# Gate products of a recurrent branch: full-array products with zero blocks, and pairs of 64-row products

## The chip, the cores and the metric

The kernel runs on one core of a Trainium2 chip. The metric is the device time of one execution in microseconds (us). The engines are named as in the profile: PE multiplies matrices, PEld is its weight load, DVE works on vectors, ACT evaluates functions and copies, POOL does small things, SP issues most transfers.

## The reference, cut to what matters

The program is one step of a two-layer backbone on 128 context tokens and 256 latent tokens (384 columns in all). Each layer has a pooling branch, an attention branch and a recurrent branch, then a feed-forward part. The change touches the two gates of the recurrent branch:

```python
xb = xf.reshape(b, l, LRU_BLOCKS, LRU_BLK)          # 8 blocks of 64 channels
rg = sigmoid(einsum('blnc,encd->eblnd', xb, wa) + ba)   # e: forward, backward
ig = sigmoid(einsum('blnc,encd->eblnd', xb, wx) + bx)
log_a = LRU_C * rg * log_sigmoid(lam)
a = exp(log_a)
inp = sqrt(-expm1(2 * log_a)) * ig * xf
hf, hb = linear_scan(a[0], inp[0]), linear_scan(a[1], inp[1], reverse)
```

Each gate is a product of a block of 64 channels with a 64 x 64 matrix. Everything is float32.

## The kernel before

Features lie on the 128 rows, tokens on the columns. A product in float32 precision is made of three products of rounded halves, `mm3` (L339): high weights by high data (L341), low weights by high data (L342), high weights by low data (L343). The weights come in chunks of 8 or 4 matrices of 128 x 128, in the order of `chunk_order` (L52). Each chunk is loaded to `raw` (L291), rounded to `whi` by ACT (L304) and its remainder is written to `wlo` by DVE (L313). Six buffers of each kind let this run ahead of the products.

Every engine works through its own instructions in the order in which the program was traced; `job` (L407) interleaves them by hand: the products of a chunk, then one stage of each evacuation that is still under way (`tick`), one step of the side work (`side_step`), then the first stage of its own evacuation, then some modulation steps on DVE (`after`, L261). PSUM has eight banks, taken in turn.

In each layer the first branch group (b = 0, the pooling branch) carries the recurrent gates. `lru_gates` (L603) is called for channel chunk c = 0, 1, 2 ahead of d = 2, 4, 6, and for c = 3 behind d = 7. Each chunk has 128 channels, so two blocks of 64. Before, the two 64 x 64 matrices of a gate stand on the diagonal of a 128 x 128 matrix whose other two quarters are zero. For each direction `e` there are two such matrices, so 2 x 3 products of 386 columns into two banks, `pa` and `px`. ACT takes both with a Tanh (L615 `th`, L616 `ti`), then computes `t2` (L619) and an Exp (L620); DVE has three operations (L622 to L624) in the next stage, ACT one more (L626) in the one after.

Behind the call for c = 3 the evacuations are flushed. Then the side work begins: `branch_lru_scan` starts with eight square roots on ACT (L634), then DVE multiplies (L648), scans (L655) and sums (L661, L662); `branch_attn` has, pair of heads by pair, transposes of v (L764), scores (L701: products of 64 rows, two heads side by side in two banks), a softmax on DVE and ACT (L714 to L736), transposes of its result (L743), copies out (ACT L749, DVE L752) and the products with v (L778, L783). The main stream of that time is the q, k and v products, whose banks ACT empties (L857).

Of the kernel before, what the change touches and what calls it, by code (L numbers as in the profile page):

```python
# [45 lines left out]
# products that warm the tensor engine up, around the first modulation vectors  # L46
WN = (8, 1, 1)
# modulation steps for each group of products, by part of the layer
# [3 lines left out]
def chunk_order():  # L52
    o = []
    for l in range(L):
        ms = [0, 1, 2, 3, 16, 17, 18, 19, 20, 21, 22, 23]
        if l == 0:
            ms = [m for m in ms if m not in FIRST0]
        o += [("in", l, m, 8) for m in ms]
        o += [("pw", l, 0, 4)]
        for b in (0, 2, 1):  # L60
            o += [("in", l, 24 + b * 8, 8)]
            for d in range(8):
                if b == 0 and d in (2, 6):
                    o += [("lru", l, d // 4, 8)]
                if d < 7:
                    o += [("in", l, 25 + b * 8 + d, 8)]
                o += [("br", l, b * 8 + d, 4)]
            if b == 0:
                for p in range(4):
                    o += [("in", l, 4 + p, 8), ("in", l, 8 + p, 8), ("in", l, 12 + p, 8)]  # L70
        o += [("wo", l, d, 8) for d in range(8)]
        for i in range(KF):
            o += [("fi", l, 2 * i, 8), ("fi", l, 2 * i + 1, 8)]
        for d in range(8):
            o += [("fo", l, 3 * d, 8), ("fo", l, 3 * d + 1, 8), ("fo", l, 3 * d + 2, 6)]
    return o
# [13 lines left out]
def emit(ctx, tc, A, outs):  # L90
# [33 lines left out]
    # silu(c), features on partitions, as the stationary side of small products  # L124
# [13 lines left out]
    # sel[p, s] = 1 where p = s modulo 32  # L138
# [3 lines left out]
    # 2h / count at the clipped ends of the pooling windows  # L142
    edge = cp.tile([128, 4, 2, 8], F32, name="edge")

    # additive mask of key columns, last column first
    cmask = cp.tile([128, 64], F32, name="cmask")

    def build_consts():
        ti = small("ti")
        G.iota(ti, pattern=[[1, 8]], base=0, channel_multiplier=0, allow_small_or_imprecise_dtypes=True)  # L150
        for g in range(4):
            h = float(1 << g)
            V.tensor_scalar(edge[:, g, 0], ti, h, None, op0=OP.add)
            V.tensor_scalar(edge[:, g, 1], ti, -1.0, 2 * h - 1, op0=OP.mult, op1=OP.add)
            yield
        V.tensor_scalar(edge[:, :, 1], edge[:, :, 1], 1.0, None, op0=OP.max)
        yield
        V.reciprocal(edge, edge)
        yield
        for g in range(4):  # L160
            V.tensor_scalar(edge[:, g], edge[:, g], 2.0 * (1 << g), None, op0=OP.mult)
            yield
        G.memset(cmask, 0.0)
        for rr in range(2):
            v = cmask[rr * 64:(rr + 1) * 64]
            # query column p, key column c = 63 - i: c >= min(p - 8, 48) and c < max(p - 8, 0) + 16
            G.affine_select(v[:, 16:64], v[:, 16:64], pattern=[[-1, 48]], base=55,
                            channel_multiplier=-1, compare_op=OP.is_ge, fill=NEG)
            G.affine_select(v[:, 0:48], v[:, 0:48], pattern=[[1, 48]], base=-56,
                            channel_multiplier=1, compare_op=OP.is_ge, fill=NEG)  # L170

    # derived per-channel parameters, both layers at once
# [3 lines left out]
    def build_dpar():  # L176
# [5 lines left out]
        # -log_sigmoid(lam) = max(-lam, 0) + log1p(z), z = exp(-|lam|)  # L182
# [13 lines left out]
        # log1p(z) = 2 atanh(z / (2 + z)), s <= 1/3  # L196
# [28 lines left out]
    def load_crow():  # L225
        # silu(c) * 2, broadcast over partitions
        Q.dma_start(out=crow, in_=A["crow"].unsqueeze(0).to_broadcast([128, 2, D]))
# [102 lines left out]
    def w_ahead(done, full=False):  # L330
        """traced before the products with the last `done` chunks, which still hold their tiles"""
        n = ws["use"] + NH - done
        w_lo(min(ws["cv"], n))
        w_hi(n)
        if full or done > 2:
            w_lo(n if full or done > 3 else n - 1)
        w_dma(min(n + NR, ws["lo"] + NR))
# [7 lines left out]
    def split_from(src, n=NT, scale=1.0, name="s"):  # L345
        """float32 data in SBUF or PSUM (times scale) -> two float32r tiles"""
        hi, lo = heap(name + "h", F32R), heap(name + "l", F32R)
        S.activation(hi[:, :n], src, AF.Copy, scale=scale)
        if isinstance(scale, float) and scale == 1.0:
            V.tensor_tensor(lo[:, :n], src, hi[:, :n].bitcast(F32), op=OP.subtract)  # L350
        else:
            V.scalar_tensor_tensor(lo[:, :n], src, scale, hi[:, :n].bitcast(F32), op0=OP.mult, op1=OP.subtract)
        return hi, lo

    def split_g(put, src, n=NT, scale=1.0, name="s"):
        """split_from in two stages"""
# [50 lines left out]
    def job(mems, mv, evac, units=1.0, full=False):  # L407
        """mems: lists of chunks, one PSUM bank for each; k outermost where there are several"""
# [25 lines left out]
    def prep_x(l, which, d, shift=True):  # L434
        """x * g (1 + sc), not yet divided by the token's rms, with the shift as two more columns"""
# [56 lines left out]
    def normed(l, which, R, mv):  # L492
        """hi and lo of h = rmsnorm(x) * g * (1 + sc) + sh, a pair of tiles per block of features"""
# [36 lines left out]
    def first_group(l, which, keys, evs, kst):  # L530
        """the first products behind a norm: from x before the division, which the evacuation makes up for"""
# [22 lines left out]
    def seg_copy(dst, offs, src):  # L554
        """PSUM (or the pair that undo gives) to the two token ranges of a padded tile"""
# [7 lines left out]
    def branch_pool(l, g, up, y):  # L563
        h = 1 << g
        st = heap("ws")
        # sliding sum over [t - h, t + h)
# [36 lines left out]
    def lru_gates(l, c, w, y):  # L603
        """one chunk of channels, both directions"""
        q = dpar[l]
        xc, mv = y.pop(("xc", c))
        for e in range(2):
            pa, px = psum(), psum()
            mm3(pa, w, (c % 2) * 4 + e * 2, mv, True, True, n=LW)
            mm3(px, w, (c % 2) * 4 + e * 2 + 1, mv, True, True, n=LW)  # L610

            def ev(pa, px, i, e):
                n = slice(0, LW)
                th, ti, t2 = heap("th"), heap("ti"), heap("t2")
                S.activation(th[:, n], pa[:, n], AF.Tanh, scale=0.5, bias=q[:, i:i + 1])  # L615
                S.activation(ti[:, n], px[:, n], AF.Tanh, scale=0.5, bias=q[:, 8 + i:9 + i])  # L616
                C, C2 = q[:, 16 + i:17 + i], q[:, 24 + i:25 + i]
                # log a = C (1 + th)
# [4 lines left out]
                V.scalar_tensor_tensor(t2[:, n], th[:, n], 1.0, t2[:, n], op0=OP.add, op1=OP.mult)       # 1 - a  # L623
                V.scalar_tensor_tensor(th[:, n], t2[:, n], 2.0, t2[:, n], op0=OP.subtract, op1=OP.mult)  # a^2 - 1  # L624
                yield
                S.activation(t2[:, n], t2[:, n], AF.Identity, scale=-1.0, bias=1.0)                      # a  # L626
                y["lru", c, e] = (t2, th, ti)
            push(ev(pa, px, e * 4 + c, e))
# [41 lines left out]
    def load_attn(l, y, p):  # L670
        for h in (2 * p, 2 * p + 1):
            t = heap("bias")
            rpb = A["rpb"]
            for rr in range(2):
                lo = 5 - rr
                # the table's last axis comes reversed; key columns are laid out from the last to the first
# [13 lines left out]
    def branch_attn(l, y):  # L690
        def scores(p, qt):
            """both heads of a pair side by side, each on its half of the rows"""
# [238 lines left out]
    def start(y):  # L931
        """modulation of the first norm on the tensor engine, beside the first products; its shift comes last"""
# [27 lines left out]
        def first_mod():  # L960
            """the first scales, one block of features at a time"""
# [76 lines left out]
        def warm(n):  # L1038
            """products of no use that keep the tensor engine's clock up while the first data comes"""
            ps = psum("warm")  # L1040
            for _ in range(n):
                T.matmul(ps[:, 0:128], ident, ident, start=True, stop=True)
# [210 lines left out]
    # the last norm, tokens on partitions  # L1253
# [24 lines left out]
def layout(i):  # L1278
# [7 lines left out]
    def fm(a):  # [..., n*128] -> [128, ...*n]  # L1286
        a = np.asarray(a).reshape(-1, 128)
        return a.T
# [11 lines left out]
    def tiles(w):  # [L, K, M] -> [L, M/128, 128(k), K/128, 128(m)]  # L1300
# [4 lines left out]
    # the first products and their modulation, in the order of their use  # L1305
# [5 lines left out]
    lru = np.zeros((L, 4, 2, 2, 128, 128), np.float32)  # L1311
    for w, name in enumerate(("lru_wa", "lru_wx")):
        a = f[name]
        for ch in range(4):
            for half in range(2):
                r = slice(64 * half, 64 * half + 64)
                lru[:, ch, :, w, r, r] = a[:, :, 2 * ch + half]
    A["lru"] = c(lru.reshape(L, 2, 8, 128, 128).transpose(0, 1, 3, 2, 4))
# [32 lines left out]
```

## Time and profile before

| | us |
|---|---|
| three runs | 1251.32, 1251.81, 1252.44 |
| median | 1251.81 |
| profiled execution, first to last instruction (span) | 1250.2 |
| mean granted TensorE clock over the span | 0.995 of full |
| PE busy | 1237.8 |
| DVE busy | 888.6 |
| ACT busy | 599.8 |

The profile is of one more execution. Only its span is given, not its own whole time; the median of the runs is 1.6 us above that span. A product of 384 columns is shown with 0.34 us, but the next one starts 0.175 us after it: products are pipelined, so starts are what counts. On ACT and DVE too the next operation begins some 0.1 us ahead of the shown end of the one before.

### The profile page before, as it was taken

What the parts mean: (1) busy time and instruction counts of PE and PEld (TensorE: products, weight loads), DVE (VectorE), ACT (ScalarE), POOL (GpSimd) and SP (SyncE); (2) the same over time, 40 slices, a digit from 0 to 9 for tenths busy, and PEclk for the clock granted to TensorE, in tenths of its full rate; (3) what the DMA queues carried; (4) which work ended last, traced back from release to release, by engine and by line L of the source; (5) the groups of instructions that cost most, each with busy time, mean ns of one, the idle gap of its engine ahead of it and who ended that gap; (6) DMA issues with size and microseconds to landing.
All of it is one profiled execution on the core that took longest, in us unless ns stands there. A gap on an engine that the chain in (4) does not pass through costs nothing.

```text
span 1250.2 us, 19496 instructions
## 1 busy us (share of the span) xinstructions
PE 1237.8 (99%) x7414; PEld 1213.4 (97%) x7414; DVE 888.6 (71%) x1650; ACT 599.8 (48%) x1095; POOL 73.0 (6%) x187
## 2 busy tenths in 40 slices
PE   8999999999999999999999999999999999999997
PEld 7799999999999999999999999999999999999997
DVE  5788798988977987756779668975676784442432
ACT  4487765534456333333347577553344743332331
POOL 0000141000200000010000013200010000000000
PEclk8999999999999999999999999999999999999999
DMA  9646676456645666646643557733554365333421
GB/s 330 239 127 211 173 146 155 142 188 209 208 129 172 237 229 206 208 137 191 210 147 103 159 168 171 143 111 118 169 186 135 116 205 168 132 108 103 121 78 51
DMA packets 65438, 204.32 MB, mean 163 GB/s; under 512 B 7744, under 2 KB 12992, under 8 KB 65216
## 3 DMA queue, kind: packets, MB, share of 16 engines
q1 hardware_dynamic: 62848, 197.82, 48.6%
q0 software_dynamic: 2496, 5.25, 4.0%
q8 instruction: 58, 0.95, 0.3%
q14 instruction: 36, 0.29, 0.1%
HBM read 200.41 MB, written 2.63 MB: 162 GB/s over the span
## 4 chain that ended last, share of the span: by engine, by line
PE 73%; issue 22%; DVE 3%; ACT 1%; DMA 0%; SPq 0%; POOLq 0%; POOL 0%; DVEq 0%
PE ps L341 23%; PE ps L343 22%; PE ps L342 22%; PE tp L743 1%; PE sc L701 1%; PE o L783 1%; DVE wlo L313 1%; PE ma L954 1%; DMA w<-in_wm 0%; PE fb L1144 0%; DVE hf L655 0%; ACT th L634 0%; DVE ti L648 0%; PE o L778 0%; ACT whi L304 0%
## 5 line engine op out<-in xcount | busy, mean ns | idle before, releaser
L341 PE MATMUL ps<-hh,whi 128*128 128x384 f32 x1320 | 447.3, 339 | 0.0
L343 PE MATMUL ps<-hl,whi 128*128 128x384 f32 x1320 | 444.5, 337 | 0.0
L342 PE MATMUL ps<-hh,wlo 128*128 128x384 f32 x1320 | 444.3, 337 | 0.0
L313 DVE TENSOR_TENSOR wlo<-raw,whi 128x1024 fp32r<-128x1024 f32 (+2 forms) x296 | 322.4, 1114 | 22.8 <-ACT whi L304 22.8
L304 ACT ACTIVATE whi<-raw 128x1024 fp32r<-128x1024 f32 (+2 forms) x296 | 280.1, 970 | 102.9 <-PE ps L343 62.0
L341 PEld LDWEIGHTS ps<-hh,whi 128*128 128x128 f32 x1320 | 247.8, 188 | 1.6 <-issue 0.3
L343 PEld LDWEIGHTS ps<-hl,whi 128*128 128x128 f32 x1320 | 247.8, 188 | 0.0
L342 PEld LDWEIGHTS ps<-hh,wlo 128*128 128x128 f32 x1320 | 247.8, 188 | 0.0
L261 DVE SCALAR_TENSOR_TENSOR junk<-wm,crow 128x1024 bf16<-128x1024 f32 x160 | 195.2, 1220 | 26.3 <-DMA wm<-in_wm 24.2
L343 PE MATMUL ps<-svl,whi 128*128 128x384 f32 x352 | 118.7, 337 | 0.0
L341 PE MATMUL ps<-svh,whi 128*128 128x384 f32 x352 | 118.6, 337 | 0.0
L905 ACT ACTIVATE ft<-ps 128x384 f32<-128x384 f32 x40 | 19.7, 492 | 206.0 <-PE ps L343 206.0
L342 PE MATMUL ps<-svh,wlo 128*128 128x384 f32 x352 | 118.3, 336 | 0.0
L890 DVE SCALAR_TENSOR_TENSOR x<-ps,modv,x 128x128 f32<-128x128 f32 x64 | 23.7, 411 | 85.2 <-PE ps L343 85.0
L907 DVE TENSOR_TENSOR ft<-ft,ps 128x384 f32<-128x384 f32 x40 | 22.0, 551 | 84.2 <-ACT ft L905 66.7
L868 ACT ACTIVATE tg<-ps 128x384 f32<-128x384 f32 x48 | 23.5, 489 | 114.5 <-PE ps L343 114.5
L343 PEld LDWEIGHTS ps<-svl,whi 128*128 128x128 f32 x352 | 66.1, 188 | 0.0
L341 PEld LDWEIGHTS ps<-svh,whi 128*128 128x128 f32 x352 | 66.1, 188 | 0.0
L342 PEld LDWEIGHTS ps<-svh,wlo 128*128 128x128 f32 x352 | 66.1, 188 | 0.0
L877 DVE SCALAR_TENSOR_TENSOR tg<-tg,ps 128x384 f32<-128x384 f32 x48 | 26.5, 551 | 53.5 <-PE ps L343 53.0
L452 ACT ACTIVATE sq<-x 128x384 f32<-128x384 f32 x40 | 20.1, 513 | 67.4 <-DVE x L890 67.4
L342 PE MATMUL ps<-mgh,wlo 128*128 128x384 f32 x128 | 43.2, 338 | 0.0
(239 smaller groups left out, 1713.0 us busy)
## 6 DMA issues: line engine op xcount, KB each, us to landing
raw<-in_in SPq DMA_DIRECT2D x90, 512.0 KB, 4.2
raw<-in_fi SPq DMA_DIRECT2D x88, 512.0 KB, 4.3
wm<-in_wm SPq DMA_DIRECT2D x80, 512.0 KB, 4.6
raw<-in_fo SPq DMA_DIRECT2D x32, 512.0 KB, 4.6
raw<-in_br SPq DMA_DIRECT2D x48, 256.0 KB, 2.9
w<-in_wm SPq DMA_DIRECT2D x16, 512.0 KB, 7.0
raw<-in_wo SPq DMA_DIRECT2D x16, 512.0 KB, 4.2
raw<-in_fo SPq DMA_DIRECT2D x16, 384.0 KB, 3.2
```

The costliest lines, as they stand in the source:

```text
L261: V.scalar_tensor_tensor(j, t, 0.5, crow[:, s], op0=OP.mult, op1=OP.mult, accum_out=modv[l][:, comp, d, s:s + 1])
L304: S.activation(hi[:, :nk], r[:, :nk], AF.Copy)
L313: V.tensor_tensor(lo[:, :nk], r[:, :nk], hi[:, :nk].bitcast(F32), op=OP.subtract)
L341: T.matmul(ps[:, :n], hi[:, k], mv[0][:, :n], start=start, stop=False)
L342: T.matmul(ps[:, :n], lo[:, k], mv[0][:, :n], start=False, stop=False)
L343: T.matmul(ps[:, :n], hi[:, k], mv[1][:, :n], start=False, stop=stop)
L452: S.activation(sq[:, :NT], xt[d], AF.Square)
L868: S.activation(t[:, :NT], ps[:, :NT], AF.Tanh, scale=0.5)
L877: V.scalar_tensor_tensor(t[:, :NT], t[:, :NT], 1.0, ps[:, :NT], op0=OP.add, op1=OP.mult)
L890: V.scalar_tensor_tensor(xt[d][:, o:o + n], ps[:, o:o + n], modv[l][:, comp, d, s:s + 1], xt[d][:, o:o + n], op0=OP.mult, op1=OP.add)
L905: S.activation(t[:, :NT], pg[:, :NT], AF.Silu)
L907: V.tensor_tensor(t[:, :NT], t[:, :NT], pu[:, :NT], op=OP.mult)
```

## The change

For each direction and chunk there are still six products, but of 64 rows each: a pair of them stands on the two halves of the array, one block of channels on each half, and goes to two banks. One product now has both gates of its block in its 128 columns: bank `pb[0]` has gate a of block 0 on rows 0 to 63 and gate x of block 0 on rows 64 to 127; bank `pb[1]` has gate x of block 1 first and gate a of block 1 behind. The weight chunk has no zero blocks and is half as long. So `th` and `ti` are each put together from two banks, 64 rows at a time: four Tanh of 64 rows instead of two of 128. The rest of the stage is the same. (The diff also takes out comments; the lines behind are shifted by 7.)

```diff
                 if b == 0 and d in (2, 6):
-                    o += [("lru", l, d // 4, 8)]
+                    o += [("lru", l, d // 4, 4)]
...
         for e in range(2):
-            pa, px = psum(), psum()
-            mm3(pa, w, (c % 2) * 4 + e * 2, mv, True, True, n=LW)
-            mm3(px, w, (c % 2) * 4 + e * 2 + 1, mv, True, True, n=LW)
+            pb = [psum(), psum()]
+            j = (c % 2) * 2 + e
+            for wi, mi in ((0, 0), (1, 0), (0, 1)):
+                for b in range(2):
+                    r = slice(64 * b, 64 * b + 64)
+                    T.matmul(pb[b][:, :LW], w[wi][r, j], mv[mi][r, :LW], start=wi + mi == 0, stop=mi == 1)
...
-                S.activation(th[:, n], pa[:, n], AF.Tanh, scale=0.5, bias=q[:, i:i + 1])
-                S.activation(ti[:, n], px[:, n], AF.Tanh, scale=0.5, bias=q[:, 8 + i:9 + i])
+                for t, o, f in ((th, 0, 0), (ti, 8, 1)):
+                    for b in range(2):
+                        r, rs = slice(64 * b, 64 * b + 64), slice(64 * (b ^ f), 64 * (b ^ f) + 64)
+                        S.activation(t[r, n], pb[b][rs, n], AF.Tanh, scale=0.5, bias=q[r, o + i:o + i + 1])
...
-    lru = np.zeros((L, 4, 2, 2, 128, 128), np.float32)
+    lru = np.zeros((L, 4, 2, 128, 128), np.float32)
...
-                lru[:, ch, :, w, r, r] = a[:, :, 2 * ch + half]
+                lru[:, ch, :, 64 * b:64 * b + 64, o:o + 64] = a[:, :, 2 * ch + b]
```

On PE, the call for c = 2 of layer 0 (`xch`, `xcl` are the halves of the data, `whi`, `wlo` those of the weights, `ps` the banks). Before, the first direction:

```order
L341 MATMUL ps_1678<-xch_1244,whi_1510 128x386
L342 MATMUL ps_1678<-xch_1244,wlo_1558 128x386
L343 MATMUL ps_1678<-xcl_1245,whi_1510 128x386
L341 MATMUL ps_1679<-xch_1244,whi_1510 128x386
L342 MATMUL ps_1679<-xch_1244,wlo_1558 128x386
L343 MATMUL ps_1679<-xcl_1245,whi_1510 128x386
```

And now (the size shown is that of the output, each reads 64 rows):

```order
L614 MATMUL ps_1686<-xch_1244,whi_1514 128x386
L614 MATMUL ps_1687<-xch_1244,whi_1514 128x386
L614 MATMUL ps_1686<-xch_1244,wlo_1566 128x386
L614 MATMUL ps_1687<-xch_1244,wlo_1566 128x386
L614 MATMUL ps_1686<-xcl_1245,whi_1514 128x386
L614 MATMUL ps_1687<-xcl_1245,whi_1514 128x386
```

The first bank was complete behind the third product; now both banks are complete only behind the last pair.

On ACT, both directions of the same call. Before:

```order
L615 ACTIVATE th_1686<-ps_1678,dpall_101 128x386
L616 ACTIVATE ti_1687<-ps_1679,dpall_101 128x386
L619 ACTIVATE t2_1688<-th_1686,dpall_101 128x386
L620 ACTIVATE th_1686<-th_1686,dpall_101 128x386
L615 ACTIVATE th_1701<-ps_1693,dpall_101 128x386
L616 ACTIVATE ti_1702<-ps_1694,dpall_101 128x386
L619 ACTIVATE t2_1703<-th_1701,dpall_101 128x386
L620 ACTIVATE th_1701<-th_1701,dpall_101 128x386
L304 ACTIVATE whi_1710<-raw_1512 128x1024
```

And now:

```order
L623 ACTIVATE th_1694<-ps_1686,dpall_101 64x386
L623 ACTIVATE th_1694<-ps_1687,dpall_101 64x386
L623 ACTIVATE ti_1695<-ps_1686,dpall_101 64x386
L623 ACTIVATE ti_1695<-ps_1687,dpall_101 64x386
L626 ACTIVATE t2_1696<-th_1694,dpall_101 128x386
L627 ACTIVATE th_1694<-th_1694,dpall_101 128x386
L623 ACTIVATE th_1711<-ps_1703,dpall_101 64x386
L623 ACTIVATE th_1711<-ps_1704,dpall_101 64x386
L623 ACTIVATE ti_1712<-ps_1703,dpall_101 64x386
L623 ACTIVATE ti_1712<-ps_1704,dpall_101 64x386
L626 ACTIVATE t2_1713<-th_1711,dpall_101 128x386
L627 ACTIVATE th_1711<-th_1711,dpall_101 128x386
```

Four operations more stand in the queue ahead of the next weight chunk; nothing else moves on ACT, and on DVE only the remainder of the gate weights is half as long.

## Rows read from the trace of the kernel before

**Rows 1.** Page, part 1: busy us, share of the span, instructions.

```profile
PE 1237.8 (99%) x7414; PEld 1213.4 (97%) x7414; DVE 888.6 (71%) x1650; ACT 599.8 (48%) x1095; POOL 73.0 (6%) x187
```

**Rows 2.** Windows: length, then busy (count) of PE, PEld, DVE, ACT, POOL.

```profile
160.00:193.70 33.70, 33.54 (x209) 32.02 (x207) 32.66 (x73) 17.65 (x41) 14.47 (x24) 1.00 0.71 145
762.00:798.00 36.00, 36.00 (x227) 34.45 (x227) 34.96 (x78) 18.50 (x42) 16.85 (x29) 1.00 0.73 139
```

**Rows 3.** Timeline, call c = 0, layer 0: start, duration, engine, line, operation.

```profile
103.87 1.22 DVE L313 TENSOR_TENSOR wlo<-raw,whi 128x1024 fp32r<-128x1024 f32 x1
103.99 0.34 PE L341 MATMUL ps<-xch,whi 128*128 128x386 f32 x1
...
106.11 0.34 PE L341 MATMUL ps<-hh,whi 128*128 128x384 f32 x1
...
106.28 0.34 PE L342 MATMUL ps<-hh,wlo 128*128 128x384 f32 x1
```

**Rows 4.** Timeline around a group of scores, layer 0 (products of 64 rows).

```profile
172.83 0.34 PE L343 MATMUL ps<-hl,whi 128*128 128x384 f32 x1
173.10 0.30 PEld L701 LDWEIGHTS sc<-k,q 64*128 64x128 f32 x4 [0.25 <-issue]
173.10 0.70 PE L701 MATMUL sc<-k,q 64*128 64x256 f32 x4
...
173.95 0.45 PE L341 MATMUL ps<-hh,whi 128*128 128x384 f32 x1
...
174.24 0.34 PE L342 MATMUL ps<-hh,wlo 128*128 128x384 f32 x1
```

**Rows 5.** Timeline of ACT, layer 0, from call c = 2 to v.

```profile
134.28 0.58 ACT L615 ACTIVATE th<-ps,dpall 128x386 f32<-128x386 f32 x1 [1.26 <-PE ps L343]
...
135.23 0.70 ACT L619 ACTIVATE t<-th,dpall 128x386 f32<-128x386 f32 x1
...
142.12 1.06 ACT L304 ACTIVATE whi<-raw 128x1024 fp32r<-128x1024 f32 x1 [0.67 <-PE ps L343]
...
144.23 1.06 ACT L304 ACTIVATE whi<-raw 128x1024 fp32r<-128x1024 f32 x1 [0.22 <-PE ps L343]
145.20 0.57 ACT L615 ACTIVATE th<-ps,dpall 128x386 f32<-128x386 f32 x1
...
146.13 0.71 ACT L619 ACTIVATE t<-th,dpall 128x386 f32<-128x386 f32 x1
...
151.09 0.53 ACT L626 ACTIVATE t<-t 128x386 f32<-128x386 f32 x1 [0.81 <-DVE th L624]
...
157.60 1.05 ACT L304 ACTIVATE whi<-raw 128x1024 fp32r<-128x1024 f32 x1
...
159.87 0.48 ACT L857 ACTIVATE v<-ps 128x384 f32<-128x384 f32 x1
```

**Rows 6.** Timeline of DVE, layer 0, two instructions.

```profile
158.68 1.23 DVE L313 TENSOR_TENSOR wlo<-raw,whi 128x1024 fp32r<-128x1024 f32 x1 [2.57 <-ACT whi L304]
...
193.31 0.42 DVE L734 TENSOR_SCALAR pr<-pr,m 128x384 f32<-128x384 f32 x1
```

**Rows 7.** Timeline of PE, layer 0: call c = 2, transposes of v, of a softmax.

```profile
133.84 0.34 PE L343 MATMUL ps<-xcl,whi 128*128 128x386 f32 x1
...
162.99 0.49 PE L764 MATMUL tp<-ident,v 128*128 128x128 f32 x3
...
193.88 0.52 PE L743 MATMUL tp<-ident,pr 128*128 128x128 f32 x3 [0.34 <-DVE pr L734]
```

**Rows 8.** Timeline, the same places in layer 1.

```profile
747.93 0.57 ACT L615 ACTIVATE th<-ps,dpall 128x386 f32<-128x386 f32 x1
...
761.40 1.23 DVE L313 TENSOR_TENSOR wlo<-raw,whi 128x1024 fp32r<-128x1024 f32 x1 [1.44 <-ACT whi L304]
...
801.61 0.28 DVE L752 COPY ptc<-tp 128x128 f32<-128x128 f32 x1
...
802.10 0.27 PE L778 MATMUL o<-ptc,vv 128*64 128x128 f32 x1
```

More of the change, by code (lines that the diff above doesn't have):

```diff
@@ L607, in lru_gates, with ev @@
         for e in range(2):
-            pa, px = psum(), psum()
-            mm3(pa, w, (c % 2) * 4 + e * 2, mv, True, True, n=LW)
-            mm3(px, w, (c % 2) * 4 + e * 2 + 1, mv, True, True, n=LW)
-            def ev(pa, px, i, e):
+            pb = [psum(), psum()]
[4 more added lines that the diff above has]
+                    T.matmul(pb[b][:, :LW], w[wi][r, j], mv[mi][r, :LW], start=wi + mi == 0, stop=mi == 1)
+            def ev(pb, i, e):
                 n = slice(0, LW)
                 th, ti, t2 = heap("th"), heap("ti"), heap("t2")
-                S.activation(th[:, n], pa[:, n], AF.Tanh, scale=0.5, bias=q[:, i:i + 1])
-                S.activation(ti[:, n], px[:, n], AF.Tanh, scale=0.5, bias=q[:, 8 + i:9 + i])
+                for t, o, f in ((th, 0, 0), (ti, 8, 1)):
+                    for b in range(2):
+                        r, rs = slice(64 * b, 64 * b + 64), slice(64 * (b ^ f), 64 * (b ^ f) + 64)
+                        S.activation(t[r, n], pb[b][rs, n], AF.Tanh, scale=0.5, bias=q[r, o + i:o + i + 1])
                 C, C2 = q[:, 16 + i:17 + i], q[:, 24 + i:25 + i]
@@ L627, in ev @@
                 y["lru", c, e] = (t2, th, ti)
-            push(ev(pa, px, e * 4 + c, e))
+            push(ev(pb, e * 4 + c, e))
     def branch_lru_scan(l, y):
@@ L1314, in layout @@
         for ch in range(4):
-            for half in range(2):
-                r = slice(64 * half, 64 * half + 64)
-                lru[:, ch, :, w, r, r] = a[:, :, 2 * ch + half]
-    A["lru"] = c(lru.reshape(L, 2, 8, 128, 128).transpose(0, 1, 3, 2, 4))
+            for b in range(2):
+                o = 64 * (b ^ w)
+                lru[:, ch, :, 64 * b:64 * b + 64, o:o + 64] = a[:, :, 2 * ch + b]
+    A["lru"] = c(lru.reshape(L, 2, 4, 128, 128).transpose(0, 1, 3, 2, 4))
     br = f["w_branch"].reshape(L, 3, 4, 128, 8, 128).transpose(0, 1, 4, 3, 2, 5)
```

## The prediction

> **What bounds the kernel now.** I read the page's busy shares first, then timelines around the gates, then those of the stage behind them. PE is busy for 99% of the span, ACT for 48%, DVE for 71% [rows 1]: over the whole, PE sets the time, and work on ACT looks free. But the shares are means. Between the end of the gates and the middle of the attention's start DVE is busy for 32.66 of 33.70 us in layer 0 and 34.96 of 36.00 us in layer 1, with ACT at half and PE just as full as DVE [rows 2]. In that stretch two engines run level. The reader should see who waits there: in layer 0 the transposes of a softmax at 193.88 stood 0.34 us for the DVE operation that ends at 193.73 [rows 6, 7]; in layer 1 DVE's copy ends at 801.89, and the last L778 product, which takes it, starts at 802.10, when PE already works on its group [rows 8]. So DVE is at its limit twice, exactly where PE stops having room. And what released DVE into this stretch is ACT: DVE stood 2.57 us for a weight chunk of ACT at 158.68, and 1.44 us at 761.40 in layer 1 [rows 6, 8]. The chain is ACT behind the gates, then DVE, then PE.
>
> **The change on PE.** A call has 12 products of 386 columns. They run from 103.99 to 106.11, 2.12 us or 0.177 each [rows 3]. Does a pair of 64-row products cost one? The scores show it: four weight loads of 64 rows take 0.30 us together, at about 0.19 each, which is possible only two at a time [rows 4]. The eight passes there, of 256 and 128 columns, end within 0.85 us (173.10 to 173.95). I take six pairs at 0.177: 1.06 us. The same rows give the price of going into that mode and out of it. In: the first score starts 0.27 behind the last full product instead of 0.175, and its weight load is not hidden, some 0.1. Out: the first full product is again some 0.1 late, and the second follows after 0.29 (173.95 to 174.24) instead of 0.175. Together about 0.4 us per call, so a call takes 1.46 and saves 0.66; eight calls save 5.3 us. The Trainium skill (TensorEngine Tiling (Array Packing), Key Properties) says that a change of the tiling mode drains the engine; without that rule the sum on PE would be 8.5, and rows 4 side with it.
>
> **The change on ACT.** Each direction gets four Tanh in place of two. Two of them take 0.95 us from start to start of what follows (134.28 to 135.23) and 0.93 in the next call (145.20 to 146.13) [rows 5], so 0.47 each. No row has an ACT operation on fewer than 128 rows. The bounds: half, 0.235, if the cost goes with the rows; and 0.58, the whole duration shown, if operations on halves of one tile don't overlap. The nearest rows are the 64-row weight loads, which cost what a full one does [rows 4], so I take 0.47. That is 1.88 us more per call, 15 us in all.
>
> **The smaller parts.** Four weight chunks are half as long; that saves ACT and DVE about half of a split each (0.5 us) and some transfer, all before the calls that matter, and PE waits for none of it. The tightest weight is that of the product behind call c = 0: its remainder is done at 105.09, PE asks for it at 106.28 [rows 3]. PE will ask 0.55 earlier (0.66 less 0.1 of the way out), so 0.6 us are left. No wait.
>
> **Where the ACT work lands.** Take the calls c = 2 and c = 3 of layer 0, which stand close together. PE comes to c = 2 by two calls earlier, 1.32 us. ACT used to start 0.44 behind the third product (133.84 to 134.28) [rows 5, 7]; now it must wait for the fifth, in the third pair, which starts about 0.2 later than the third product did, so ACT starts 1.1 us earlier. Then it has eight more Tanh until the end of c = 3: 3.76 us. It used to stand twice for PE in between, 0.67 and 0.22 [rows 5]; PE is earlier there, so these 0.89 go. The third gap, 0.81 at 151.09, is a wait for DVE, which itself waits for the Exp on ACT, so it moves along. Sum: 3.76 - 1.1 - 0.89 = **1.75 us later** at the end of the gates. Queued behind are the square roots, the evacuations of q, k and v and three weight chunks, all 1.75 us later.
>
> Two engines wait for these. PE comes to the transposes of v at 162.99 - 2.64 = 160.35; v was done at 160.35 [rows 5, 7] and now comes at 162.1: the first wait, some 1.75 us. And DVE gets the chunk that ACT split at 157.60 at 160.4 instead of 158.68 [rows 5, 6]. From there to 193.73 DVE has no idle time to catch up with [rows 2], so its result comes at 195.5, and the transposes that were waiting for it at 193.88 [rows 7] start **1.75 us later than before**, although PE had been 2.64 us ahead. PE's whole gain of the layer ends in waits, and 1.75 more. Behind that, all engines are late by the same amount at most, so nothing is added, and PE, again the only bound, can't make it up.
>
> Layer 1 has the same order, 602.73 us later (747.93 against 145.20) [rows 5, 8], and the same lack of room: DVE is busy throughout [rows 2] and PE's value products at 802 wait for its copy [rows 8]. Again 1.75.
>
> **Sum.** 2 x 1.75 = 3.5 us on the profiled span of 1250.2, so 1253.7; the median of the runs is 1.6 above that span, which gives **1255.3 us**. The sign hangs on one price. With x for the time of one 64-row Tanh, a layer is late by 16x - 3.76 - 2.0, so 0 at x = 0.36. At 0.58 it is 3.5 per layer, 1258.8. At 0.235 ACT no longer adds anything and starts each call when PE lets it, 2.0 us earlier by c = 3; a layer then gains those 2.0 (DVE still sets the end) and the time is 1247.8.
>
> A rule bears on this. The rows say that ACT behind the gates releases DVE, and DVE releases PE [rows 6, 7]. The Trainium skill (TensorEngine Tiling (Array Packing), PSUM Bottleneck) says that tiling speeds up TensorE but not the evacuation of PSUM, which may become the bottleneck; by it PE's 5.3 us are not the sum, and here the evacuation even grows.
>
> **The rivals.**
>
> *Faster: ACT's price goes with rows, or PE's time alone counts.* The mechanism: each half Tanh costs well under 0.36, ACT follows PE, and the gain survives: 1247.8 as worked out. PE alone, with no wait at all, would be 1251.8 - 5.3 = 1246.5. For it: PE is 99% busy and ACT 48% [rows 1]. Against it: DVE's full stretch and the two places where PE already waits for DVE [rows 2, 6 to 8]; and nothing shows a price by rows. The same page of the skill (Theoretical Speedup) gives up to twice the speed for a contraction of 64 or less; read alone, it would stand for this rival.
>
> *No change to be measured.* The lag is partly absorbed. In layer 0 the row at 193.88 shows the wait itself; in layer 1 I read it only from the order of two rows. If layer 1 had room for DVE's lag, it would keep what v leaves: 2.64 - 1.75 = 0.9 gained, and the sum would be 1.75 - 0.9 = +0.85: 1252.7. A Tanh of 0.28 to 0.44 also ends within 2.5 us of the old time.
>
> *Much slower: the pairs don't run side by side.* The change would then not do what it says: 12 products at 0.177 plus 0.4, a call 0.4 longer. ACT would start c = 2 about 1.35 later instead of 1.1 earlier, the end of c = 3 would lag by 1.35 + 3.76 - 0.89 = 4.2, and two layers make 8.4: 1260.2. It decides as soon as the second product of a pair starts 0.1 or more behind the first. Against it stand the scores, of the same shape [rows 4]; for it only that these are of another number type.
>
> **How the numbers follow.** A measurement of this kernel tells about 0.2%, 2.5 us, from no change. Forecast 0.58, and within it 1253 to 1258.8 by the bounds of the Tanh, of which perhaps a fifth lies under 2.5 us; the absorbed lag 0.16; the faster rival 0.16; serial pairs 0.10. Slower: 0.46 + 0.10 and some of the edges, 0.58. Same: 0.12 + 0.13 = 0.25. Faster: 0.17. The range reaches from 1247.5, which takes in the faster bound, to 1258.8, and leaves out serial pairs and PE alone.
>
> **What would show it.** Right: call c = 0 takes about 1.46 us on PE, the two products of a pair starting within 0.01; four 64-row Tanh some 0.47 apart; ACT some 15 us busier (less two for the half chunks); the last evacuation of the gates ends 1.5 to 2 us later against the old timetable in layer 0; PE idle at the transposes of v with ACT as releaser (1 to 2 us, twice), and at softmax transposes or value products with DVE as releaser; PE with 5 us less work but some 8 to 9 us of gaps in all. Wrong: 64-row Tanh well under 0.4 apart, or PE without gaps at L764 and L743 in the new kernel; then ACT's extra work was free and the time falls. Also wrong if the Tanh for c = 2 start much earlier or later than 1.1 us ahead of the old time, which would mean that the price of the pairs is off.

## The result and the profile after

The changed kernel takes 1259.94 us (median of 4, 1259.79 to 1260.25), the kernel before, in the same series, 1251.89: 1.0068 times as long, 95% interval 1.0056 to 1.0079. That is slower by 8.05 us, where 3.5 was forecast, and 1.1 us outside the range. The profiled span is 1258.2 against 1250.2.

The page of the changed kernel, part 1 (busy us, share of the span, instructions):

```profile
PE 1238.8 (98%) x7414; PEld 1209.1 (96%) x7414; DVE 887.2 (71%) x1650; ACT 618.4 (49%) x1127; POOL 72.8 (6%) x187
```

Against [rows 1] ACT has 18.6 us more; the shares look the same, and that is the trap of this case. PE's busy time did not fall by 5 us but rose by 1.0; why is told with the clock below.

What PE does in call c = 0 of layer 0, in the timeline (start, duration, engine, line, operation; x2 is the pair). First the last product ahead of the call in the kernel before:

```profile
103.81 0.34 PE L343 MATMUL ps<-yal,whi 128*128 128x384 f32 x1
```

And in the changed kernel, from the same product on:

```profile
104.08 0.34 PE L343 MATMUL ps<-yal,whi 128*128 128x384 f32 x1
104.35 0.45 PE L614 MATMUL ps<-xch,whi 64*128 64x386 f32 x2
104.64 0.34 PE L614 MATMUL ps<-xch,wlo 64*128 64x386 f32 x2
...
105.35 0.34 PE L614 MATMUL ps<-xcl,whi 64*128 64x386 f32 x2
105.61 0.44 PE L341 MATMUL ps<-hh,whi 128*128 128x384 f32 x1
105.89 0.34 PE L342 MATMUL ps<-hh,wlo 128*128 128x384 f32 x1
```

A pair is shown with 0.34 us, as one product is, and four steps from pair to pair take 0.71 (104.64 to 105.35), 0.177 each: a pair costs one product. From the last product ahead of the call to the second one behind it are 1.81 us (104.08 to 105.89); before, it was 2.47 (103.81 to 106.28 [rows 3]). The call saves some 0.66 us.

This profiled execution was already 0.27 us late at the last product ahead of the call (104.08 against 103.81), where nothing of the change had run yet. Times that are set against the old timetable below contain these 0.27 us.

ACT in the timeline of the changed kernel, from call c = 2 to v:

```profile
133.43 1.19 ACT L623 ACTIVATE th<-ps,dpall 64x386 f32<-64x386 f32 x2 [1.46 <-PE ps L614]
...
135.86 0.71 ACT L626 ACTIVATE t<-th,dpall 128x386 f32<-128x386 f32 x1
...
145.98 1.17 ACT L623 ACTIVATE th<-ps,dpall 64x386 f32<-64x386 f32 x2
...
154.80 0.53 ACT L633 ACTIVATE t<-t 128x386 f32<-128x386 f32 x1 [0.81 <-DVE th L631]
...
161.30 1.04 ACT L304 ACTIVATE whi<-raw 128x1024 fp32r<-128x1024 f32 x1
...
163.56 0.48 ACT L864 ACTIVATE v<-ps 128x384 f32<-128x384 f32 x1
```

Four Tanh take 2.43 us (133.43 to 135.86), so 0.605 each, where two of 128 rows took 0.95 [rows 5]. ACT starts call c = 2 0.85 us earlier than before (1.12 if the 0.27 are taken off), call c = 3 0.78 later, and the last evacuation of the gates 3.71 later (154.80 against 151.09). Chunk and v are as late: 161.30 against 157.60, 163.56 against 159.87 [rows 5].

DVE in the timeline, the two instructions that answer to [rows 6]:

```profile
162.38 1.23 DVE L313 TENSOR_TENSOR wlo<-raw,whi 128x1024 fp32r<-128x1024 f32 x1 [2.56 <-ACT whi L304]
...
197.03 0.42 DVE L741 TENSOR_SCALAR pr<-pr,m 128x384 f32<-128x384 f32 x1
```

They come 3.70 and 3.72 us late. And PE, which stood at the transposes of v and then again at those of the softmax [rows 7]:

```profile
160.46 0.34 PE L343 MATMUL ps<-hl,whi 128*128 128x384 f32 x1
164.09 0.90 PE L771 MATMUL tp<-ident,v 128*128 128x128 f32 x3 [3.29 <-ACT v L864]
...
167.42 0.52 PE L342 MATMUL ps<-hh,wlo 128*128 128x384 f32 x1
167.74 0.52 PE L343 MATMUL ps<-hl,whi 128*128 128x384 f32 x1
...
197.60 0.52 PE L750 MATMUL tp<-ident,pr 128*128 128x128 f32 x3 [0.41 <-DVE pr L741]
```

PE was 2.35 us ahead of the old timetable, so with the 0.27 four calls saved 2.62 us, 0.655 each. It waits 3.63 from start to start, and the softmax transposes come 3.72 us late (193.88 to 197.60). Behind the wait the products stand 0.32 apart instead of 0.175: the clock. In windows over the wait and the stretch behind it, layer 0 and layer 1 (length; busy us and count of PE, PEld, DVE, ACT, POOL; granted TensorE clock; DMA share; GB/s):

```profile
160.00:175.00 15.00, 11.71 (x59) 10.66 (x58) 12.38 (x22) 9.10 (x17) 6.41 (x11) 0.77 0.76 162
766.00:782.00 16.00, 12.69 (x62) 11.64 (x61) 14.35 (x26) 9.44 (x18) 6.73 (x12) 0.79 0.77 185
```

Before, the clock stood at 1.00 there [rows 2]. From 164.09 to 169.50 it stood at 0.50, the lower of its two levels, 1.2 GHz. The slow products also explain PE's busy time: in experiment 2 below, with the same products at full clock, it is 1232.9 us.

So two chains end at the softmax transposes of layer 0. PE was 1.10 us late at the transposes of v (162.99 to 164.09) and 3.66 behind the slow products; DVE's result was 3.72 late. In layer 1 it is different. The same softmax transposes in the kernel before:

```profile
796.00 0.49 PE L743 MATMUL tp<-ident,pr 128*128 128x128 f32 x3
```

And in the changed kernel the transposes of v and those of the softmax:

```profile
770.55 0.90 PE L771 MATMUL tp<-ident,v 128*128 128x128 f32 x3 [3.31 <-ACT v L864]
...
803.95 0.49 PE L750 MATMUL tp<-ident,pr 128*128 128x128 f32 x3
```

PE comes to the transposes of v 4.87 us late (765.68 before), loses 3.1 us more at the lower clock, and is 7.95 late at the softmax transposes without having waited for DVE. There the wait for v and the clock set the end.

### The profile page after: what moved, and what is told of

The parts are those of the page before. It is cut to its first block, busy times and chain, and to the rows that moved or that the text cites. A ratio compares the mean times of both kernels' runs of the same rounds, so it can differ in the third digit from the quotient of the medians.

```text
span 1258.2 us, 19548 instructions
## 1 busy us (share of the span) xinstructions
PE 1238.8 (98%) x7414; PEld 1209.1 (96%) x7414; DVE 887.2 (71%) x1650; ACT 618.4 (49%) x1127; POOL 72.8 (6%) x187
## 4 chain that ended last, share of the span: by engine, by line
PE 69%; issue 22%; ACT 4%; DVE 2%; DMA 1%; SPq 0%; POOL 0%; POOLq 0%; DVEq 0%; ACTq 0%
PE ps L341 21%; PE ps L343 21%; PE ps L342 21%; PE tp L750 1%; PE sc L708 1%; PE o L790 1%; ACT whi L304 1%; ACT ti L623 1%; ACT th L623 1%; PE ma L961 1%; DVE wlo L313 1%; ACT th L641 1%; PE ps L614 1%; DMA w<-in_wm 0%; ACT t L626 0%
## 5 line engine op out<-in xcount | busy, mean ns | idle before, releaser
L341 PE MATMUL ps<-mgh,whi 128*128 128x384 f32 x128 | 43.2, 338 | 0.0
```

What stands on the lines that cost most here:

```text
L341: T.matmul(ps[:, :n], hi[:, k], mv[0][:, :n], start=start, stop=False)
```

## The experiments

The theory (A): the four Tanh per direction cost ACT far more than assumed, its queue makes v and DVE's weight chunks late by that, and DVE's full stretch carries it to PE; the pairs themselves are a gain.

**1. Half Tanh alone.** The kernel before, full products, but each Tanh in two halves of 64 rows:

```diff
-S.activation(th[:, n], pa[:, n], AF.Tanh, scale=0.5, bias=q[:, i:i + 1])
-S.activation(ti[:, n], px[:, n], AF.Tanh, scale=0.5, bias=q[:, 8 + i:9 + i])
+for t, ps, o in ((th, pa, 0), (ti, px, 8)):
+    for b in range(2):
+        r = slice(64 * b, 64 * b + 64)
+        S.activation(t[r, n], ps[r, n], AF.Tanh, scale=0.5, bias=q[r, o + i:o + i + 1])
```

> The kernel before, full products, but each of the two Tanh of a gate evacuation split into two of 64 rows (same bank, same rows in and out). Theory A (a 64-row Tanh simply costs 0.605 us from start to start instead of 0.47, and the queue on ACT carries it to DVE and PE): Tanh 0.60 apart; between the call c = 2 and the end of c = 3 16 x 0.605 - 8 x 0.47 - 0.89 = 5.0 us more on ACT per layer, which DVE passes on to PE; about 1262 us (1251.9 + 10), PE waits at the transposes of v about 2.4 us. Theory B (the price comes from the pairs: two banks written side by side, or rows that cross over): Tanh 0.47 apart, 2.9 us per layer, about 1257.6 us.

Measured: 1262.32 us against 1251.6 (ratio 1.0086, interval 1.0071 to 1.0101). The timeline:

```profile
133.58 1.17 ACT L618 ACTIVATE th<-ps,dpall 64x386 f32<-64x386 f32 x2 [1.26 <-PE ps L343]
...
135.97 0.71 ACT L621 ACTIVATE t<-th,dpall 128x386 f32<-128x386 f32 x1
...
164.73 0.69 PE L766 MATMUL tp<-ident,v 128*128 128x128 f32 x2 [2.27 <-ACT v L859]
```

0.60 each (133.58 to 135.97), with no product changed and no half moved to other rows. The halves alone make more than the whole loss.

**2. Pairs without halves.** The changed kernel with two whole Tanh, each on one bank. It leaves out the sorting of the halves, so its outputs are not those of the reference; the products are the same:

```diff
-for t, o, f in ((th, 0, 0), (ti, 8, 1)):
-    for b in range(2):
-        r, rs = slice(64 * b, 64 * b + 64), slice(64 * (b ^ f), 64 * (b ^ f) + 64)
-        S.activation(t[r, n], pb[b][rs, n], AF.Tanh, scale=0.5, bias=q[r, o + i:o + i + 1])
+for t, o, b in ((th, 0, 0), (ti, 8, 1)):
+    S.activation(t[:, n], pb[b][:, n], AF.Tanh, scale=0.5, bias=q[:, o + i:o + i + 1])
```

> The changed kernel with the pairs of products, but each bank taken by one Tanh of 128 rows as before; this leaves out the putting together of the gates (the halves of the two gates of block 1 and the gate x of block 0 end in the wrong places). Theory A: what made the change slower is the four Tanh alone; the pairs save 0.65 us per call, ACT starts each call earlier and has no more to do than before; a layer gains what ACT and DVE let through, 2.0 us of PE's 2.6; about 1247.9 us, no wait of PE at v. Theory C (the pairs themselves do harm, or DVE's stretch does not move with ACT): 1251.9 us or more.

Measured: 1247.21 us against 1251.6 (0.9966, 0.9954 to 0.9979). PE goes from the last product, at 159.31, into the transposes of v without a gap:

```profile
159.49 0.49 PE L769 MATMUL tp<-ident,v 128*128 128x128 f32 x3
```

So the pairs are worth 4.4 of the 5.2 us that eight calls save (8 x 0.655), and the loss comes with the halves.

**3. A price list.** The kernel before, with groups of six Tanh of one kind behind its last output:

```diff
+def half(k, rs, rd, n=386, src=None):
+    s = yb[k % 2] if src is None else src
+    S.activation(u[k % 3][rd, :n], s[rs, :n], AF.Tanh, scale=0.5, bias=bi[rd, 0:1])
...
+for k in range(6):
+    half(k, lo, lo)
...
+for k in range(6):
+    half(k, (lo, hi)[k % 2], (lo, hi)[k % 2])
```

> The kernel before with a price list of Tanh on ACT behind the last output (six of a kind: 128 rows; rows 0 to 63; 64 to 127; the two halves in turn; 32 rows; 96 rows; 128 columns at 128 and 64 rows; from SBUF at 128 and 64 rows). The time grows by some 40 us for the list alone. Theory A1 (any operation on fewer than 128 rows loses the overlap with the next one): 0.60 us from start to start at 64, 32 and 96 rows alike, 0.47 at 128. Theory A2 (it is the change of rows from one operation to the next): 0.47 for 64 rows in a row on the same half, 0.60 only for the halves in turn.

The whole time, 1285.75 us, says nothing here. In the timeline the first and the last of six on rows 0 to 63, then of six with the halves in turn:

```profile
1247.61 0.59 ACT L1282 ACTIVATE u<-yt,dpall 64x386 f32<-64x386 f32 x1
...
1249.93 0.61 ACT L1282 ACTIVATE u<-yt,dpall 64x386 f32<-64x386 f32 x1
...
1259.14 0.58 ACT L1282 ACTIVATE u<-yt,dpall 64x386 f32<-64x386 f32 x1
...
1262.12 0.58 ACT L1282 ACTIVATE u<-yt,dpall 64x386 f32<-64x386 f32 x1
```

Five steps in 2.32 us, 0.465 each, on fixed rows; five in 2.98, 0.60 each, in turn. A Tanh of 64 rows costs what one of 128 does; what costs is the change of rows: then the next operation no longer starts before the shown end of the one ahead. The first reading, "fewer rows, no overlap" (A1), falls.

**4. Pairs where ACT has room.** The changed kernel with pairs in calls c = 0 and 1, full products and whole Tanh in c = 2 and 3:

```diff
-            j = (c % 2) * 2 + e
+            if c < 2:
+                j = c * 2 + e
...
+            else:
+                for g in range(2):
+                    mm3(pb[g], w, (c - 2) * 4 + e * 2 + g, mv, True, True, n=LW)
...
+                    if c >= 2:
+                        S.activation(t[:, n], pb[f][:, n], AF.Tanh, scale=0.5, bias=q[:, o + i:o + i + 1])
+                        continue
```

> The pairs only in the calls c = 0 and c = 1 of each layer; c = 2 and c = 3 with full products and two whole Tanh as before. Theory A (the damage is done where two calls stand close together at the end of the gates; behind c = 0 and c = 1 ACT has room to catch up before c = 2): ACT starts c = 2 1.3 us earlier and stays so; DVE and PE move with it; 1251.9 - 2 x 1.3 = 1249.3 us, faster than both. Theory D (any extra ACT work in the gates is passed on): slower than before, about 1255 us.

Measured: 1248.95 us against 1251.6 (0.9977, 0.9967 to 0.9986). It is faster than both kernels: four calls keep their 2.6 us, with the same halves on ACT, because there ACT's longer gates fall into time in which it waited for PE: ahead of call c = 2 (the evacuation at 131.58 before) that wait was 3.57 us before, and 0.19 here.

**5. Another order of the halves.** First those that write rows 64 to 127:

```diff
-for t, o, f in ((th, 0, 0), (ti, 8, 1)):
-    for b in range(2):
+for b in (1, 0):
+    for t, o, f in ((th, 0, 0), (ti, 8, 1))[::1 if b else -1]:
```

> The changed kernel with the same four Tanh per direction in another order: first the two that write rows 64 to 127, then the two that write rows 0 to 63. The price list of the third experiment had 0.465 from start to start for 64 rows as for 128 as long as all stand on the same rows, and about 0.60 when the halves take turns. In the changed kernel each direction has four such changes (rows 0 to 63, 64 to 127, again 0 to 63, again 64 to 127, then all rows), 0.60 instead of 0.47 each. Theory A2-out (the rows that are written count): two changes are left per direction, so 0.27 us less per direction, four directions stand ahead of v in calls c = 2 and c = 3, so about 1.1 us per layer: 1257.7 us, the wait of PE at the transposes of v 2.6 instead of 3.6 us. Rival A2-in (the rows that are read count too): the bank rows still alternate, four changes stay, 1259.9. Rival A1 (a Tanh on fewer rows is slower by itself): 1259.9 as well, with all four 0.60 apart.

Measured: 1260.11 us against 1251.31 (1.007, 1.0057 to 1.0084): no gain, a miss for A2-out. The last three of the four Tanh of a direction and what follows, in the timeline:

```profile
133.75 1.19 ACT L623 ACTIVATE ti<-ps,dpall 64x386 f32<-64x386 f32 x2
134.96 0.58 ACT L623 ACTIVATE th<-ps,dpall 64x386 f32<-64x386 f32 x1
135.57 0.71 ACT L626 ACTIVATE t<-th,dpall 128x386 f32<-128x386 f32 x1
```

Still 0.60 apart (133.75 to 134.96, two steps). In this order the rows that are read change each time, as A2-in has it. (The step behind the fourth, 0.61, goes to an operation that reads the fourth's result, so it tells nothing of rows.)

**6. Which rows.** The same list with read and written rows changed apart:

```diff
+for k in range(6):
+    half(k, (lo, hi)[k % 2], lo)
...
+for k in range(6):
+    half(k, lo, (lo, hi)[k % 2])
...
+for k in range(6):
+    half(k, lo, hi)
```

> The kernel before with a second price list behind its last output, six operations of a kind: Tanh on 128 rows; read rows in turn (0 to 63, 64 to 127), written rows always 0 to 63; read always 0 to 63, written in turn; read 0 to 63 and written 64 to 127 throughout; 128 and 64 rows in turn, both from row 0; three on rows 0 to 63, then three on 64 to 127; lists on 128 rows between them; then on DVE 128 rows, rows 0 to 63, rows 64 to 127, halves in turn, 128 rows. Theory A2-out: 0.60 only where the written rows change, 0.465 in the list with read rows in turn, in the crossing list and in that of 128 and 64 rows; one change in the list of three and three. A2-in: 0.60 also in the list with read rows in turn. On DVE no row shows a price; if DVE has the same rule, its halves in turn stand about 0.13 further apart than its lists on fixed rows. Whole time about 1288, which says nothing.

The whole time was 1295.17 us, 7 more than expected. First and last of six on ACT: read in turn, written in turn, read 0 to 63 and written 64 to 127 throughout:

```profile
1247.36 0.59 ACT L1282 ACTIVATE u<-yt,dpall 64x386 f32<-64x386 f32 x1
...
1250.40 0.58 ACT L1282 ACTIVATE u<-yt,dpall 64x386 f32<-64x386 f32 x1
...
1253.81 0.58 ACT L1282 ACTIVATE u<-yt,dpall 64x386 f32<-64x386 f32 x1
...
1256.79 0.57 ACT L1282 ACTIVATE u<-yt,dpall 64x386 f32<-64x386 f32 x1
...
1260.37 0.57 ACT L1282 ACTIVATE u<-yt,dpall 64x386 f32<-64x386 f32 x1
...
1262.70 0.58 ACT L1282 ACTIVATE u<-yt,dpall 64x386 f32<-64x386 f32 x1
```

0.61, 0.60 and 0.47 per step: a change of either costs some 0.13 us; a crossing that stays the same costs nothing. (The rows of the bias go with the written ones in these lists, as in the kernel; which of the two counts is not told apart. 128 and 64 rows in turn, both from row 0, also stood 0.465 apart.) On DVE, 128 rows, then the halves in turn:

```profile
1277.31 0.56 DVE L1309 TENSOR_SCALAR u<-yt 128x386 f32<-128x386 f32 x1 [32.40 <-ACT u L1282]
...
1279.66 0.55 DVE L1309 TENSOR_SCALAR u<-yt 128x386 f32<-128x386 f32 x1
...
1285.99 0.55 DVE L1309 TENSOR_SCALAR u<-yt 64x386 f32<-64x386 f32 x1
...
1288.88 0.56 DVE L1309 TENSOR_SCALAR u<-yt 64x386 f32<-64x386 f32 x1
```

0.47 against 0.58: DVE has the same price. The Trainium skill (VectorE: DVE Perf Modes, Two Vector instructions with no wait between them) says of DVE that an instruction whose inputs or output start in another group of 32 rows than the last access to that memory starts only when all earlier ones have finished; the DVE list agrees (0.58 is the whole duration shown, 0.55, and a little), and the ACT lists look the same (0.60 against a shown 0.58). In the changed kernel all four Tanh of a direction differ in where they read or where they write, so each of them pays this price, and no order of the four avoids it.

**7. The clock.** The changed kernel, with useless products where PE waits for v:

```diff
+for _ in range(12 if p == 0 else 0):
+    T.matmul(tp[:, 0:128], ident, ident, start=True, stop=True)
```

> The changed kernel with twelve useless products of the identity, some 2.5 to 3 us, ahead of the first transposes of v of each layer, where PE waits 3.6 us for ACT. They are overwritten by the transposes. Theory B (PE's idle time is what made the granted clock fall to half behind the wait): the wait shrinks to under 1.2 us, the granted clock stays at 1.00 in both stretches behind it (0.77 and 0.79 in the changed kernel), layer 0 ends no earlier because DVE sets the end there, and layer 1 gives back the 0.7 us that the slow products cost: 1259.2 us. If the clock cost more than I read, down to 1257. Rival (the clock falls for another reason): stretches at 0.77 to 0.79 as before, 1259.9 or somewhat more. Rival (the bank of the transposes is not free in time): the products start late themselves and the time grows by up to 3 us per layer.

Measured: 1258.94 us against 1251.31 (1.0059, 1.0046 to 1.0073). Timeline of PE, then the windows of layer 0 and 1:

```profile
160.47 2.84 PE L771 MATMUL tp<-ident 128*128 128x128 f32 x24
163.96 0.55 PE L773 MATMUL tp<-ident,v 128*128 128x128 f32 x3 [0.65 <-ACT v L866]
...
197.46 0.52 PE L750 MATMUL tp<-ident,pr 128*128 128x128 f32 x3 [0.75 <-DVE pr L741]
...
802.63 0.52 PE L750 MATMUL tp<-ident,pr 128*128 128x128 f32 x3 [0.37 <-DVE pr L741]
```

```profile
160.00:175.00 15.00, 14.35 (x100) 13.41 (x98) 12.49 (x23) 8.86 (x17) 6.45 (x11) 1.00 0.74 167
766.00:782.00 16.00, 15.34 (x105) 14.40 (x104) 14.32 (x26) 9.02 (x17) 6.46 (x11) 1.00 0.79 186
```

The clock stays at 1.00, so PE's wait is what lowered it. Yet in layer 0 the softmax transposes come at 197.46, 3.58 us late instead of 3.72, and this execution was 0.17 less late ahead of the gates: nothing is gained, because PE, now faster, waits longer for DVE. That DVE sets the end of this stretch is shown. In layer 1 the softmax transposes come at 802.63, 6.63 us late instead of 7.95, and now they too wait for DVE; behind the value products that follow PE is 6.99 late (802.96 before) against 7.69. So the clock costs something in layer 1 alone, as expected, and that is small: the time is 1.0 us below that of the changed kernel, but only 0.4 if each is taken against its own runs of the kernel before, and the intervals overlap.

**8. Relief for ACT, first try.** The order of 5, and the Identity behind the gates on POOL:

```diff
-S.activation(t2[:, n], t2[:, n], AF.Identity, scale=-1.0, bias=1.0)
+G.tensor_scalar(t2[:, n], t2[:, n], -1.0, 1.0, op0=OP.mult, op1=OP.add)
```

> The changed kernel with the order of the Tanh as in the first kernel of this call, and with the Identity behind the gates (one per direction, 0.47 us of ACT from start to start, and a wait of 0.81 us of ACT for DVE ahead of the one at 151.09 in the kernel before) on POOL, which is idle for 94% of the span. Theory A (ACT's queue at the end of the gates is the cost, PE's saving is real): ACT's lag at v, 3.5 us in the changed kernel, falls by 1.1 for the order, 4 x 0.47 for the Identity of the last four directions and 0.8 for the wait, to about -0.3, so PE does not wait at v and keeps a good part of 2.6 us per layer; since DVE sets the end of layer 0's stretch, 1 to 1.5 us per layer stay: about 1249.5 us, faster than both kernels. Rival (the cost is elsewhere in the pairs): 1257 or more. Rival (an operation on POOL of 128 x 386 takes long, or slows DVE): the scans wait for it and it ends between 1251 and 1257.

Measured: 1269.49 us against 1251.31 (1.0145, 1.0131 to 1.0159), far from the 1249.5 forecast, and not by anything in the pairs, as the rival of 1257 and more would have it. The timeline of POOL and PE:

```profile
158.58 0.60 POOL L689 DMA_DIRECT2D ckv<-in_ckv  x1
...
161.88 0.55 PE L771 MATMUL tp<-ident,v 128*128 128x128 f32 x3 [1.14 <-ACT v L864]
...
169.22 0.80 PE L708 MATMUL sc<-ckv,q 64*128 64x128 f32 x4 [6.16 <-DMA ckv<-in_ckv]
```

The wait for v shrank as expected (3.29 to 1.14), and a new one of 6.16 us took its place (9.05 in layer 1). On POOL the transfers of the attention stand behind the Identities, which wait for DVE; the keys' cache was asked for at 158.58, in the changed kernel at 144.54. I had looked at POOL's busy share and not at what was queued there.

**9. Relief for ACT, second try.** The changed kernel, with the Identities on POOL but issued at the head of the scan stage, behind those transfers:

```diff
-                yield
-                S.activation(t2[:, n], t2[:, n], AF.Identity, scale=-1.0, bias=1.0)
...
                 a, nb, gi = y["lru", c, e]
+                G.tensor_scalar(a[:, :LW], a[:, :LW], -1.0, 1.0, op0=OP.mult, op1=OP.add)
```

> The changed kernel, its Tanh in their own order, with the eight Identity operations of a layer on POOL, but issued only behind the gates, at the head of the scan stage, so that POOL's transfers for the attention stand ahead of them and not behind (that was what the kernel with both edits lost: ckv was asked for 14 us later). ACT loses three Identities of 0.43 us each among the last four directions, and at the end one with its wait: the next chunk starts 0.62 behind the last Exp (152.86) instead of at 155.23, so 1.75 more. Of the 3.5 us by which ACT comes late to v some 0.5 to 1.3 are left. Theory A (the time follows ACT's lag at the end of the gates, microsecond for microsecond and per layer): 1251.5 plus 2 x 0.5 to 1.3, and less loss of clock, so about 1253.5 (1252.5 to 1254.5), with PE's gap at the transposes of v 1 to 2 us instead of 3.6. Rival (the pairs cost something that does not run over ACT): 1257 or more. Rival (POOL's operations slow DVE or keep the scans waiting): the gap at v shrinks, and yet the time stays above 1256.

Measured: 1253.68 us against 1251.43 (1.0017, 1.0008 to 1.0027).

```profile
160.06 0.48 ACT L863 ACTIVATE v<-ps 128x384 f32<-128x384 f32 x1
160.59 0.55 PE L770 MATMUL tp<-ident,v 128*128 128x128 f32 x3 [0.76 <-ACT v L863]
...
194.15 0.52 PE L749 MATMUL tp<-ident,pr 128*128 128x128 f32 x3 [0.75 <-DVE pr L740]
```

6 of the 8 us are gone with nothing done to pairs or halves. (This execution began 0.7 us ahead of that before: against it v is some 0.9 late, the softmax transposes 1.0, the time 2.25, two layers.) The time follows ACT's lag, as A has it, and the wait of 8 was the queue on POOL.

**10. Three calls in pairs, Identities on POOL.** The edits of 4, up to c = 2, and of 9 (the lines shown are against 4):

```diff
-            if c < 2:
-                j = c * 2 + e
+            if c < 3:
+                j = c % 2 * 2 + e
```

> Pairs in calls c = 0, 1 and 2, full products for c = 3, and the Identities on POOL behind the gates. Theory A: the four directions of c = 0, 1 cost ACT only time in which it waited for PE; c = 2 costs 2.94 us on ACT, of which 1.17 (earlier start) and 0.89 (former waits) are covered; the Identities give back 2 to 2.4. So ACT comes to v earlier than in the kernel before, PE does not wait at v, and three calls of 0.65 us per layer stay: 1251.5 - 3.9 = 1247.6, or 1248.3 where DVE holds it up by 0.3 per layer at the softmax. It would be the fastest of the kernels with the reference's output. Rival (lags of ACT add up as in the changed kernel): gaps at v, 1251 or more.

Measured: 1249.08 us against 1251.43 (0.998, 0.9971 to 0.9989). No wait at v, but no better than 4: the third call's gain is kept in layer 0 and given back in layer 1. There PE was 3.83 us ahead of the old timetable behind the third call, and is 3.01 ahead at the softmax transposes (796.00 before), which now wait for DVE:

```profile
792.99 0.52 PE L756 MATMUL tp<-ident,pr 128*128 128x128 f32 x3 [0.34 <-DVE pr L747]
```

The forecast of 1247.6 was 1.5 us too low, the 1248.3 with DVE's wait 0.8.

**11. The control.** The kernel before with the edit of 9 alone.

> The control for both: the kernel before with nothing but the Identities on POOL behind the gates. ACT is some 2 us earlier at v, DVE with it, but PE works without a gap there already; only the 0.34 us wait at the softmax transposes of layer 0 can go: 1251.2, no change that can be measured. If it is faster by more than 1.5 us, ACT held up PE in the kernel before as well, and what the other two kernels gain is not the pairs'. If it is slower, POOL's operations cost DVE or the scans something.

Measured: 1251.61 us against 1251.43 (1.000, 0.9991 to 1.0009), as expected. In the kernel before it gains nothing to take the eight Identities of a layer off ACT; they count only where ACT's queue has become the last to end.

## Why the prediction was wrong in size and right in kind

- **PE, right.** 0.66 per call forecast, 0.655 measured, with the way into the mode and out of it (0.27 and 0.28 where 0.175 is usual, twice each) at the 0.4 us read from the scores. The rule of the Trainium skill (TensorEngine Tiling (Array Packing), Key Properties) that a change of mode drains the engine agrees with these four steps.
- **The price of a half Tanh, wrong.** The step that failed is the sentence "The nearest rows are the 64-row weight loads, which cost what a full one does [rows 4], so I take 0.47." Alone a half does cost 0.465; but the four of a direction change rows each time, and one costs 0.605. The condition of the upper bound, no overlap, is what came true, and the bound of 0.58 itself was a little low. Call c = 3 grew by 2.93 us (145.98 to 154.80, 8.82, against 145.20 to 151.09, 5.89) where 1.88 was forecast.
- **The sum of a layer, right in form.** Forecast: 3.76 for the Tanh, less 1.1 for the earlier start and 0.89 for waits that go, 1.75. Measured against the old timetable in layer 0: 2 x 2.93, less 0.85 and 1.30, 3.71; less the 0.27 us that were there ahead of the first call, 3.44. (ACT needs 12.55 us from the start of call c = 2 to that of c = 3, before 10.92: 1.63 more, so 1.30 of waits went if c = 2 grew by the same 2.93.) The price of the Tanh alone is 2.10 too low; the earlier start is as forecast (1.12 without the 0.27), and 0.41 more of waits go.
- **The way to PE, right in layer 0, half right in layer 1.** In layer 0 ACT is 3.69 us late at v, DVE 3.72 at the softmax, PE 3.72, as the chain had it, and both waits of PE stand where they were forecast. In layer 1 only the wait for v does: PE came to the softmax transposes 7.95 late through that wait and the lower clock, with no wait for DVE. The forecast wait for DVE appears there once the clock stays up (experiment 7). Experiments 2, 4, 9 and 7 show the chain's parts.
- **The clock, missed.** That a wait of PE has a price of its own was not in the sum. The slow products made PE 2.6 us later in layer 0 and 3.1 in layer 1, but most of that lies where PE would have waited for DVE anyway; by experiment 7 it is 0.4 to 1.0 us in all. For the same reason PE's busy time did not fall by the 5 us that were to show the forecast right.
- **The total.** With 0.605 for x the prediction's own formula, 16x - 3.76 - 2.0, makes a layer 3.92 late and the time 1259.6, against 1259.94 measured. That it comes so near is in part luck: in layer 0 the lag from the first call on is 3.45 us, less than 3.92, and the clock, which the formula leaves out, adds in layer 1.
- **The rivals.** The much slower one gave 1260.2, almost the time measured, but by serial pairs; the rows of call c = 0 refute it. A time that fits is not a cause. The faster one was true of PE's part (experiment 2) and fell with the halves. That of no change, a lag partly absorbed in layer 1, fell too: both layers pass it on, at full clock as well (experiment 7, 3.58 us late behind layer 0 and 6.99 in layer 1).

## What to carry to other kernels

When an edit takes work from the bounding engine and gives more pieces to another, price the pieces in the order in which they stand: halves of a tile that take turns cost more than the same halves in a row. Make such an edit where the other engine waits anyway; here the four calls of that kind kept all of the 2.6 us that they save. Before an operation goes to an idle engine, look at what is queued behind it there.

## What was not expected of the hardware

- On ACT an operation of 386 columns starts 0.465 us behind the last one on 32, 64, 96 or 128 rows alike, and about 0.60 behind it when the first row read, or the first row written and that of the bias, has changed between 0 and 64; on DVE 0.467 and about 0.58.
- Behind a wait of PE of 3.6 us its clock stood at the lower level for some 5.4 us (0.50 from 164.09 to 169.50); with the same wait filled with products it stayed at 1.00. In experiment 1 a wait of 2.6 us did so in layer 0 (0.77 in the window of 15 us behind it) and not in layer 1 (1.00); why the two differ stays open.
